# A hybrid decoder layer on one core: two weight tiles at the start, later scales, four products out, two weight tiles kept

## The chip, the cores and the metric

The kernel runs on one core of one Trainium2 chip. A core has five engines that each work through a queue of their own: TensorE (PE: matrix products; PEld is its loading of the stationary operand), VectorE (DVE), ScalarE (ACT), GpSimd (POOL) and SyncE (SP, which issues most transfers here). They wait for each other through semaphores, and 16 DMA engines carry the transfers. The metric is the time of one execution on the device in microseconds (us), smaller is better.

## The reference

One layer of a decoder, 1024 positions by 1024 channels, in float32:

```python
h = rms_norm(x, g_mix)
va, ga, xb, gb, sa, sb = split(h @ w_in + b_in)         # 1024, 1024, 1536, 1536, 1024, 1024 columns
u = silu(layer_norm(causal_conv31(va * sigmoid(ga)), ln_g, ln_b))
y_a = u @ w_a_out
v = rg_lru(causal_conv4(xb), ...)                       # gated linear recurrence along the positions
y_b = (v * gelu(gb)) @ w_b_out
x = x + (sigmoid(sa) * y_a + sigmoid(sb) * y_b) @ w_o
f = square(relu(rms_norm(x, g_mlp) @ w_1))              # 4096 columns
out = rms_norm(x + f @ w_2, g_final)
```

In rms_norm each row is divided by the root of its mean square and multiplied by a gain per channel. The decay of the recurrence needs softplus(-lam), a vector of 1536 values.

## The kernel before, in words

Activations lie with channels on the 128 partitions and positions along the free axis, so a product has a 128x128 weight block as its stationary operand and 512 positions moving. To keep float32 accuracy every operand is split into a high part (rounded to fp32r, suffix h) and a low part (the rest, suffix l), and each product is made three times: high by high ("hh"), low weight by high activation ("lh"), high weight by low activation ("hl").

The program has stages: the first three tiles of `w_in` (written out by hand, the code shown below), the rest of `w_in`, with a scheme of seven products in place of eight for some pairs of tiles (called z products from line 900 on), the output projections, the MLP's up projection (seven products again, numbered 1 to 7, in `up_step`), and its down projection. Inside a `manual_schedule` block the order on TensorE, VectorE and ScalarE is the order of the code; later stages keep clocks of their own (`at`, `later`, `fill`) by which VectorE's work is placed between the rest. Every engine works strictly in its order.

*The start.* SyncE loads a small vector of gains (`gmix`), the first weight tile `w0`, the first half of the positions of x transposed (four tiles `xc`, two blocks of 128 channels each), then `w1`, `w2`, and then x itself with positions on partitions (`x4` to `x7`, the first half of the positions; then the second half of `xc`, then `x0` to `x3`). TensorE runs idle passes (`idle_mm`, each float32 pass of 128x128 counting as two instructions in the trace). ScalarE makes `w0`'s high part and `xh`, VectorE the low parts, and TensorE multiplies as they come: all of tile z0 (24 products), then z1, then z2, always for the first half of the positions. These first products use x times the gain alone, without the root mean square, which is multiplied in later.

*The scales.* The root mean squares of the second half in time come from `x4` to `x7`: `x_square` squares a tile and sums along its row (on ScalarE, line 195), `x_root` turns the four sums into reciprocal roots on VectorE and ScalarE (v at line 202, diagonal matrices `rd` at 208 and 210), and `x_spread` spreads them over all partitions by four products with a matrix of ones (line 217, eight instructions in the trace). `x_scaled` then scales `xc` by that and ScalarE makes the next `xh` of it. In the same place `decay_on(n)` puts the next n steps of the softplus on VectorE, small operations of 12 columns on `sm` (lines 273 to 299).

*Guard products.* In the z products, banks b and e of a pair are first written by a ScalarE copy of another bank and then added to by products. For the first two pairs `z_bank` has a product write each of these banks ahead of the copy (line 918); nothing reads what it wrote.

*The up weights.* Tile i of the MLP's up projection uses two weight tiles of 512 KB, `w_{2i}` and `w_{2i+1}` (`raws[i, 0]`, `raws[i, 1]`). The stage ahead of it reads `raws[i, 0]` for i = 0 to 3, as the left operand of seven-product tiles named gu, gs ("u" in `g_lhs`). For i = 2 and 3 `g_lhs` forgets the tile afterwards, and the loop over the tiles loads whatever is missing:

```python
up_load(i, [m_ for m_ in (0, 1) if (i, m_) not in raws])
```

A split of an up weight is made by ScalarE and by an accumulating transfer that GpSimd issues (`split_dma`, line 66: `o<-s`).

Of the kernel before, what the change touches and what calls it, by code (L numbers as in the profile page):

```python
# [30 lines left out]
def trunk_kernel(ctx: ExitStack, tc: tile.TileContext, x, xt_in, xt_eo, vecs, w_in, w_a_out, w_b_pl, w_b_sq,  # L31
                 w_rg, w_o, w_1, w_2, g_final, out):

    nc = tc.nc
# [19 lines left out]
    HALVES = (slice(0, HS), slice(HS, S))  # L54


    def load_w(w, name):

        raw = wp.tile(list(w.shape), F32, tag="raw", name=name + "_raw")
        nc.sync.dma_start(raw, w)  # L60
        return raw
# [56 lines left out]
    wp = stage.enter_context(tc.tile_pool(name="weights", bufs=2))  # L118
# [8 lines left out]
    vec = cp.tile([P, 448], F32, name="vec")  # L127

    gmix = cp.tile([P, 16], F32, name="gmix")
    nc.sync.dma_start(gmix[:, 0:8], vecs[:, 0:8])  # L130
    nc.gpsimd.dma_start(vec, vecs)
    gmix_c = gmix[:, 0:8]
    bin_c = vec[:, 8:64]
# [11 lines left out]
    xt, xc, raw0 = [], [], []  # L145
# [6 lines left out]
    def load_xc(hf, c2):  # L152
        a = T(f"xc{hf}{c2}")
        nc.sync.dma_start(a, xt_in[hf, c2])
        xc.append(a)

    def load_w0(i):
        if i < 2:
            raw0.append(load_w(w_in[(16, 0, 8)[i]], f"w{i}"))
        else:  # L160
            raw0.append(T(f"w{i}_raw").rearrange("p (k c) -> p k c", c=P))
            nc.sync.dma_start(raw0[i], w_in[(16, 0, 8)[i]])

    load_w0(0)
    for c2 in range(4):
        load_xc(0, c2)
    load_w0(1)
    load_w0(2)
    for t in range(4, 8):
        load_x(t)  # L170
# [2 lines left out]
    for t in range(4):  # L173
# [3 lines left out]
    xh = [[(X1 if hf == 0 and c2 < 2 else T)(f"xh{hf}{c2}", F32R) for c2 in range(4)]  # L177
          for hf in range(2)]
    xl = [[T(f"xl{hf}{c2}", F32R) for c2 in range(4)] for hf in range(2)]

    def xpart(a, hf, c):
        return a[hf][c // 2][:, HALVES[c % 2]]

    rs_x = {}

    def x_square(t, eng):

        hf, i = divmod(t, 4)
        if hf not in rs_x:
            rs_x[hf] = cp.tile([P, 5, 4], F32, tag="st4", name=f"stx{hf}", bufs=2)  # L190
        a, ss = xt[(t + 4) % 8], rs_x[hf][:, 0, i:i + 1]
        if eng is nc.vector:
            nc.vector.scalar_tensor_tensor(a, a, 1.0, a, ALU.mult, ALU.mult, accum_out=ss)
        else:
            nc.scalar.activation(a, a, AF.Square, accum_out=ss)
# [16 lines left out]
    def x_spread(hf):  # L212

        rb[hf] = rb["tile"][:, HALVES[hf]]
        for i in range(4):
            d = slice(i * P, (i + 1) * P)
            nc.tensor.matmul(rb[hf][:, d], ones, rb["d"][:, d], start=True, stop=True)
# [6 lines left out]
    def x_plain(c):  # L224

        u = xc[c // 2][:, HALVES[c % 2]]
        nc.scalar.activation(xpart(xh, 0, c), u, AF.Copy, scale=gmix_c[:, c:c + 1])

    def x_plain_low(c):
        u, h = xc[c // 2][:, HALVES[c % 2]], xpart(xh, 0, c)  # L230
        nc.vector.scalar_tensor_tensor(xpart(xl, 0, c), u, gmix_c[:, c:c + 1], h.bitcast(F32),
                                       ALU.mult, ALU.subtract)
# [8 lines left out]
    w0 = []  # L241

    def first_w(i, part):
        if part == "h":
            if i < 2:
                wh = wp.tile([P, 8, P], F32R, tag="wh", name=f"w{i}_h")
                wl = wp.tile([P, 8, P], F32R, tag="wl", name=f"w{i}_l")
            else:
                wh, wl = (T(f"w{i}_{n}", F32R).rearrange("p (k c) -> p k c", c=P) for n in "hl")
            w0.append((wh, wl))  # L250
            z0.append(PS(f"z{16 + i}"))
            nc.scalar.activation(wh, raw0[i], AF.Copy)
        else:
            nc.vector.tensor_tensor(w0[i][1], raw0[i], w0[i][0].bitcast(F32), ALU.subtract)

    def first_z(i, hf, k, which):
        w, a = {"hh": (0, xh), "lh": (1, xh), "hl": (0, xl)}[which]
        nc.tensor.matmul(z0[i][:, HALVES[hf]], w0[i][w][:, k, :], xpart(a, hf, k),  # L258
                         start=k == 0 and which == "hh",
                         stop=k == 7 and which == ("hl" if i == 0 else "lh"))  # L260
# [69 lines left out]
    def decay_on(n=99):  # L330

        for _ in range(n):
            next(decaying, None)

    with tc.manual_schedule(engines={mybir.EngineType.Activation, mybir.EngineType.DVE,
                                     mybir.EngineType.PE}):
        warm = cp.tile([P, 10], F32, name="warm")
        nc.vector.memset(warm[:, 0:2], 1.0)
        nc.scalar.activation(warm[:, 0:1], warm[:, 1:2], AF.Sqrt)

        spare = PS("spare", "ps2")

        def idle_mm(n):
            for _ in range(n):
                nc.tensor.matmul(spare[:, 0:P], ones, ones, start=True, stop=True)

        idle_mm(13)
        rb["tile"] = PS("rb", "ps2")
        first_w(0, "h")
        first_w(0, "l")  # L350
        for c in range(8):
            x_plain(c)
            x_plain_low(c)
            if c == 7:
                first_w(1, "h")
                first_w(1, "l")
            for which in ("hh", "lh", "hl"):
                first_z(0, 0, c, which)
        for k in range(8):
            first_z(1, 0, k, "hh")  # L360
            first_z(1, 0, k, "hl")
        decay_on(6)
        first_w(2, "h")
        first_w(2, "l")
        decay_on(14)
        for t in range(4, 8):
            x_square(t, nc.scalar)
        for k in range(8):
            first_z(1, 0, k, "lh")
        x_root(1)  # L370
        decay_on(5)
        for k in range(8):
            first_z(2, 0, k, "hh")
            first_z(2, 0, k, "hl")
            if k == 4:
                x_spread(1)
        for k in range(8):
            first_z(2, 0, k, "lh")

        for c in range(9):  # L380
            if c < 8:
                x_scaled(1, c)
            else:
                x_root(0)
                x_spread(0)
            if 3 <= c < 7:
                x_square(c - 3, nc.scalar)
# [399 lines left out]
    for i in range(2, NZ):  # L787
        n = zseq.index((i, 1))
# [20 lines left out]
    with tc.manual_schedule(engines=ENGINES):  # L809
        for s in range(3, NC1):  # L810
# [30 lines left out]
            c = CH[s - 1]  # L841
# [27 lines left out]
            for d in range(5):  # L869
                if s - d in EXP:  # L870
# [6 lines left out]
                    t = 3 * g + d - (2 if g < 3 else 1)  # L877
# [21 lines left out]
    wp = stage.enter_context(tc.tile_pool(name="weights2", bufs=3, reuse_waits="tile"))  # L899
# [13 lines left out]
    hgd = dp.tile([12, P, S], F32, name="hgd")  # L913
    def z_bank(i, b):
        zb[i, b] = t = zp.tile([P, HS], F32, tag="z", name=f"z{i}{b}")
        if i < 2 and b in "be":

            nc.tensor.matmul(t, xh[0][0][:, 0:P], xh[0][0][:, 0:HS], start=True, stop=True)
        return t

    def z_mm(i, p):
# [101 lines left out]
    with tc.manual_schedule(engines=ENGINES):  # L1023
# [159 lines left out]
        for n in range(len(zseq) + 2):  # L1183
# [9 lines left out]
            if n + 3 < len(zseq):  # L1193
                i, p = zseq[n + 3]
# [15 lines left out]
    wp = early.enter_context(tc.tile_pool(name="weights3", bufs=7, reuse_waits="tile"))  # L1210
# [191 lines left out]
    def g_lhs(w, i, p):  # L1402
        if w == "u":
            src = raws[i, 0][:, 4 * (p - 1):4 * p, :]
            if p == 2 and i > 1:
                del raws[i, 0]
        elif p in (5, 6):
            src = gs[w, i][p - 5 and 1]
        else:
            src = graw[w, i, {1: 0, 2: 1, 3: 1, 7: 0, 4: 1}[p]][:, int(p == 4)]  # L1410
        go[w, i, p] = o = T(f"g{w}{i}_{p}", F32R).rearrange("p (x k c) -> p x k c", x=2, c=P)
        if w == "a" and p in (1, 2, 7):
            nc.scalar.activation(o[:, 0], src, AF.Copy)
# [242 lines left out]
    raws = {}  # L1656
# [300 lines left out]
    with tc.manual_schedule(engines={mybir.EngineType.Activation, mybir.EngineType.DVE,  # L1957
                                     mybir.EngineType.PE}):
        for n in range(len(useq)):
# [4 lines left out]
            while ready < min(len(useq), n + look + 1):  # L1964
                i, p = useq[ready]
# [167 lines left out]
    with tc.manual_schedule(engines={mybir.EngineType.Activation, mybir.EngineType.DVE,  # L2133
                                     mybir.EngineType.PE}):
        for n, (g, p, kk) in enumerate(dseq[:-2]):
# [41 lines left out]
            if (g, m - 4) in XADD:  # L2177
                k = XADD[g, m - 4]
# [103 lines left out]
```

## Time and profile before

| | us |
|---|---|
| median of three runs (lowest, highest) | 1531.57 (1530.81, 1531.60) |
| the profiled execution | 1531.15 |
| its span, first to last instruction | 1529.4 |
| TensorE busy | 1519.5, 99%, 6722 instructions |
| VectorE busy | 1200.0, 78%, 1636 instructions |
| ScalarE busy | 928.3, 61%, 1299 instructions |
| GpSimd busy | 192.3, 13%, 228 instructions |

The granted TensorE clock is 0.999 of full speed over the span. In a timeline a row gives the start, the duration, the engine, the line, the operation, out<-in, the shape, and in brackets how long the engine stood idle before it and what released it. Successive matmuls overlap, so the distance between their starts says more than their duration. A row of the DMA view names the queue's transfers, their number and size and the median time from issue to landing.

### The profile page before, as it was taken

To read this page: it belongs to the slowest core of one execution; us is meant where nothing else is said; L and a number is where in the kernel's file an instruction comes from. 1 tells how busy PE (TensorE), PEld (TensorE's weight loads), DVE (VectorE), ACT (ScalarE), POOL (GpSimd) and SP (SyncE) were. 2 spreads that over 40 slices of the span, in tenths; PEclk is the share of its full clock that TensorE was granted. 3 is DMA by queue.
4 is the path that set the end of the run, shared out by engine and by line. 5 is a ranking of instruction groups with operands and counts; after the bars stand their busy time and mean duration, and the time that the engine had idled before them with its cause. 6 is when DMAs were issued, how large, how long until landed. Compare 5 with 4: busy or idle time off the path is not lost.

```text
span 1529.4 us, 18963 instructions
## 1 busy us (share of the span) xinstructions
PE 1519.5 (99%) x6722; PEld 1251.2 (82%) x6722; DVE 1200.0 (78%) x1636; ACT 928.3 (61%) x1299; POOL 192.3 (13%) x228
## 2 busy tenths in 40 slices
PE   9999999999999999999999999999999999999998
PEld 7878887888888888888888887888888888888886
DVE  6899996998999997788869879755555387777777
ACT  6748688576566667645575777554444455545475
POOL 0111011022222222000022332000000000101010
PEclk9999999999999999999999999999999999999999
DMA  9766779797997889964879897333333974776465
GB/s 352 188 146 154 184 159 204 196 258 209 265 261 173 186 207 271 297 226 119 269 201 302 188 205 195 138 122 111 111 111 111 302 265 131 177 211 169 107 123 153
DMA packets 130799, 296.53 MB, mean 194 GB/s; under 512 B 12896, under 2 KB 34912, under 8 KB 130704
## 3 DMA queue, kind: packets, MB, share of 16 engines
q1 hardware_dynamic: 98960, 215.92, 42.0%
q0 software_dynamic: 31600, 79.15, 28.1%
q8 instruction: 52, 0.85, 0.2%
q14 instruction: 43, 0.35, 0.1%
q10 hardware_dynamic: 144, 0.26, 0.0%
HBM read 149.79 MB, written 60.82 MB: 138 GB/s over the span
## 4 chain that ended last, share of the span: by engine, by line
PE 96%; issue 2%; DVE 1%; POOL 1%; DMA 0%; ACT 0%; POOLq 0%; ACTq 0%
PE z L725 16%; PE z L258 2%; PE d1b L2002 2%; PE d2b L2002 2%; PE d0b L2002 2%; PE d3b L2002 2%; PE d0e L2002 1%; PE d3e L2002 1%; PE d3a L2002 1%; PE d2e L2002 1%; PE d2a L2002 1%; PE d1e L2002 1%; PE d1a L2002 1%; PE d0a L2002 1%; PE rg L532 1%
## 5 line engine op out<-in xcount | busy, mean ns | idle before, releaser
L725 PE MATMUL z<-xh,win_h 128*128 128x512 f32 x368 | 115.4, 391 | 0.0
L725 PE MATMUL z<-xl,win_h 128*128 128x512 f32 x368 | 114.9, 390 | 0.0
L637 DVE SCALAR_TENSOR_TENSOR y<-u,vec,y 128x511 f32<-128x511 f32 (+14 forms) x120 | 88.2, 735 | 0.0
L725 PE MATMUL z<-xh,win_l 128*128 128x512 f32 x368 | 87.4, 389 | 0.0
L637 DVE SCALAR_TENSOR_TENSOR yt<-u,vec,yt 128x511 f32<-128x511 f32 (+6 forms) x112 | 82.5, 736 | 0.0
L637 DVE SCALAR_TENSOR_TENSOR y<-yt,csum,y 128x511 f32<-128x511 f32 (+6 forms) x112 | 82.4, 736 | 0.0
L725 PEld LDWEIGHTS z<-xh,win_h 128*128 128x128 f32 x368 | 69.1, 188 | 16.0 <-ACT win_h L67 0.5
L725 PEld LDWEIGHTS z<-xl,win_h 128*128 128x128 f32 x368 | 69.1, 188 | 14.9
L725 PEld LDWEIGHTS z<-xh,win_l 128*128 128x128 f32 x368 | 69.1, 188 | 14.6
L542 ACT ACTIVATE g<-rg,vec 96x1024 f32<-96x1024 f32 x32 | 35.5, 1110 | 72.9 <-PE rg L534 72.8
L1697 ACT ACTIVATE o<-s 128x512 fp32r<-128x512 f32 x56 | 33.7, 623 | 45.7 <-DVE s L1681 26.4
L66 POOL DMA_DIRECT2D zo<-zw x45 | 39.2, 871 | 133.8 <-ACT zo L65 110.4
L483 DVE SCALAR_TENSOR_TENSOR v<-xb,vec,v 128x1023 f32<-128x1023 f32 (+2 forms) x36 | 46.2, 1282 | 6.3 <-ACT v L474 5.3
L66 POOL DMA_DIRECT2D db_10l<-br x4 | 3.5, 877 | 339.6 <-DMA br<-in_w_dram 254.4
L66 POOL DMA_DIRECT2D win_l<-win_raw x23 | 20.0, 868 | 194.0 <-ACT win_l L65 155.9
L65 ACT ACTIVATE zo<-zw 128x512 fp32r<-128x512 f32 x45 | 28.2, 626 | 24.3 <-PE z10f L929 2.1
L1219 DVE TENSOR_TENSOR o<-s,o 128x512 fp32r<-128x512 f32 x56 | 37.2, 683 | 1.3 <-ACT o L1697 1.3
L66 POOL DMA_DIRECT2D zo<-zs x30 | 26.4, 879 | 75.9 <-ACT zo L65 63.8
L67 ACT ACTIVATE zo<-zw 128x512 fp32r<-128x512 f32 x45 | 27.9, 621 | 0.0
L578 DVE TENSOR_TENSOR_SCAN g<-a,g 128x1024 f32<-128x1024 f32 x12 | 27.5, 2291 | 0.4
L66 POOL DMA_DIRECT2D ga<-gsa x8 | 7.0, 874 | 161.0 <-DMA m<-mbd 150.8
L1219 DVE TENSOR_TENSOR o<-w_raw,o 128x512 fp32r<-128x512 f32 x38 | 25.9, 683 | 0.0
(3182 smaller groups left out, 4912.0 us busy)
## 6 DMA issues: line engine op xcount, KB each, us to landing
w_raw<-in_w_dram SPq DMA_DIRECT2D x34, 512.0 KB, 5.7
br<-in_w_dram SPq DMA_DIRECT2D x32, 512.0 KB, 6.1
ar<-fd SPq DMA_DIRECT2D x32, 512.0 KB, 7.0
zw<-in_w_in_dram SPq DMA_DIRECT2D x28, 512.0 KB, 6.9
win_raw<-in_w_in_dram SPq DMA_DIRECT2D x23, 512.0 KB, 5.0
win_l<-win_raw POOLq DMA_DIRECT2D x23, 512.0 KB, 5.2
zo<-zw POOLq DMA_DIRECT2D x45, 256.0 KB, 5.7
gates<-zg SPq DMA_DIRECT2D x32, 256.0 KB, 4.1
```

Of the source, the lines that this page charges most:

```text
L65: nc.scalar.activation(l, src, AF.Copy, scale=-1.0)
L66: nc.gpsimd.dma_start(l, src, accum_op=ALU.add)
L67: nc.scalar.activation(h, src, AF.Copy)
L258: nc.tensor.matmul(z0[i][:, HALVES[hf]], w0[i][w][:, k, :], xpart(a, hf, k), start=k == 0 and which == "hh", stop=k == 7 and which == ("hl ...
L483: nc.vector.scalar_tensor_tensor(v[:, d:S], a[:, 0:S - d], cbw_c[:, w * 12 + t:w * 12 + t + 1], v[:, d:S], ALU.mult, ALU.add)
L542: nc.scalar.activation(a, gps.pop((n, gi))[:HD, :], AF.Sigmoid, bias=(ba_c, bx_c)[gi][:, n:n + 1])
L578: nc.vector.tensor_tensor_scan(i, a, i, 0.0, ALU.mult, ALU.add)
L637: nc.vector.scalar_tensor_tensor(o[:, k:], a[:, 0:HS - k], c, o[:, k:], ALU.mult, add)
L725: nc.tensor.matmul(zps[s][:, HALVES[hf]], w[:, k, :], xw[k][part][hf], start=n == 0, stop=n == 23)
L1219: tt(l, src, h.bitcast(F32), ALU.subtract)
L1697: nc.scalar.activation(o[:, 0], src, AF.Copy)
L2002: nc.tensor.matmul(o, a, b, start=start and n == 0, stop=stop and n == len(todo) - 1, skip_group_check=not start or not stop)
```

## The change

There are four groups of edits.

1. *Loads and first products.* `w0`, `w1` and the first `xc` tile are loaded in halves; `gmix` and the first half of `xc00` are issued by ScalarE. The idle passes go from 13 to 10 calls. Weights `w0` and `w1` are split by halves, and z0's and z1's products are interleaved, two blocks of channels at a time.
2. *Scales.* The square of `x6` is made by VectorE, the squares stand ahead of `decay_on(14)`, and the spread of the first scales stands after all 16 hh and hl products of z2 instead of after ten.
3. *Guard products.* The product in `z_bank` is gone.
4. *Up weights.* `g_lhs` keeps `raws[2, 0]` and `raws[3, 0]`, so tiles `w_4` and `w_6` aren't loaded a second time.

```diff
-    nc.sync.dma_start(gmix[:, 0:8], vecs[:, 0:8])
...
-    load_w0(0)
-    for c2 in range(4):
-        load_xc(0, c2)
-    load_w0(1)
+    def half_w0(i, n):
+        k = slice(4 * n, 4 * n + 4)
+        nc.sync.dma_start(raw0[i][:, k], w_in[(16, 0)[i], :, k])
+
+    half_w0(0, 0)
+    nc.scalar.dma_start(xc[0][:, HALVES[0]], xt_in[0, 0, :, HALVES[0]])
+    nc.scalar.dma_start(gmix[:, 0:8], vecs[:, 0:8])
+    nc.sync.dma_start(xc[0][:, HALVES[1]], xt_in[0, 0, :, HALVES[1]])
+    half_w0(1, 0)
+    load_xc(0, 1)
+    half_w0(0, 1)
+    half_w0(1, 1)
+    load_xc(0, 2)
+    load_xc(0, 3)
     load_w0(2)
     for t in range(4, 8):
         load_x(t)
...
-    def x_square(t, eng):
+    def x_square(t, dve=False):
...
-        if eng is nc.vector:
+        if dve:
             nc.vector.scalar_tensor_tensor(a, a, 1.0, a, ALU.mult, ALU.mult, accum_out=ss)
         else:
             nc.scalar.activation(a, a, AF.Square, accum_out=ss)
...
+    def first_half(i, n):
+        k = slice(4 * n, 4 * n + 4)
+        h, l = (a[:, k] for a in w0[i])
+        nc.scalar.activation(h, raw0[i][:, k], AF.Copy)
+        nc.vector.tensor_tensor(l, raw0[i][:, k], h.bitcast(F32), ALU.subtract)
...
-        idle_mm(13)
+        idle_mm(10)
         rb["tile"] = PS("rb", "ps2")
         first_w(0, "h")
-        first_w(0, "l")
+        first_w(1, "h")
+        first_half(0, 0)
         for c in range(8):
             x_plain(c)
             x_plain_low(c)
-            if c == 7:
-                first_w(1, "h")
-                first_w(1, "l")
+            if c == 1:
+                first_half(1, 0)
+            elif c == 3:
+                first_half(0, 1)
+                first_half(1, 1)
             for which in ("hh", "lh", "hl"):
                 first_z(0, 0, c, which)
-        for k in range(8):
-            first_z(1, 0, k, "hh")
-            first_z(1, 0, k, "hl")
+            if c % 2:
+                for k in (c - 1, c):
+                    first_z(1, 0, k, "hh")
+                    first_z(1, 0, k, "hl")
         decay_on(6)
         first_w(2, "h")
         first_w(2, "l")
+        for t in range(4, 8):
+            x_square(t, t == 6)
         decay_on(14)
-        for t in range(4, 8):
-            x_square(t, nc.scalar)
         for k in range(8):
             first_z(1, 0, k, "lh")
         x_root(1)
         decay_on(5)
         for k in range(8):
             first_z(2, 0, k, "hh")
             first_z(2, 0, k, "hl")
-            if k == 4:
+            if k == 7:
                 x_spread(1)
         for k in range(8):
             first_z(2, 0, k, "lh")
...
     def z_bank(i, b):
         zb[i, b] = t = zp.tile([P, HS], F32, tag="z", name=f"z{i}{b}")
-        if i < 2 and b in "be":
-
-            nc.tensor.matmul(t, xh[0][0][:, 0:P], xh[0][0][:, 0:HS], start=True, stop=True)
         return t
...
             src = raws[i, 0][:, 4 * (p - 1):4 * p, :]
-            if p == 2 and i > 1:
-                del raws[i, 0]
```

Lines of the kernel after are shifted by some 15 to 16 from before. On VectorE, where the scales are made (`sm` are the steps of the decay, `stx` the sums and roots), before:

```order
L254 TENSOR_TENSOR w_l<-w_raw,w_h 128x1024
L286 SCALAR_TENSOR_TENSOR sm<-sm 128x12
L288 SCALAR_TENSOR_TENSOR sm<-sm 128x12
L290 MEMSET sm 128x12
L293 TENSOR_TENSOR sm<-sm 128x12
...
L293 TENSOR_TENSOR sm<-sm 128x12
L202 TENSOR_SCALAR stx_261<-stx_261 128x4
```

and after:

```order
L264 TENSOR_TENSOR w_l<-w_raw,w_h 128x1024
L202 SCALAR_TENSOR_TENSOR x_112,stx_251<-x_112 128x1024
L302 SCALAR_TENSOR_TENSOR sm<-sm 128x12
L304 SCALAR_TENSOR_TENSOR sm<-sm 128x12
L306 MEMSET sm 128x12
L309 TENSOR_TENSOR sm<-sm 128x12
...
L309 TENSOR_TENSOR sm<-sm 128x12
L211 TENSOR_SCALAR stx_251<-stx_251 128x4
```

The square of x6 (`x_112`) has come in ahead of the 14 decay steps, of which the first four and the last are shown; the first step of the roots (v, line 202 before, 211 after) stands behind them as it did.

On TensorE, at the end of z2's first half (`z_244` before, `z_248` after), before:

```order
L258 MATMUL z_244<-xh_131,w_h 128x512
L258 MATMUL z_244<-xl_139,w_h 128x512
L217 MATMUL rb<-rd_281,ones 128x128 x4
L258 MATMUL z_244<-xh_131,w_h 128x512
L258 MATMUL z_244<-xl_139,w_h 128x512
...
L258 MATMUL z_244<-xh_132,w_h 128x512
L258 MATMUL z_244<-xl_140,w_h 128x512
L258 MATMUL z_244<-xh_129,w_l 128x512 x2
```

and after:

```order
L274 MATMUL z_248<-xh_135,w_h 128x512
L274 MATMUL z_248<-xl_143,w_h 128x512
L226 MATMUL rb<-rd_285,ones 128x128 x4
L274 MATMUL z_248<-xh_132,w_l 128x512 x2
L274 MATMUL z_248<-xh_133,w_l 128x512 x2
L274 MATMUL z_248<-xh_134,w_l 128x512 x2
L274 MATMUL z_248<-xh_135,w_l 128x512 x2
L274 MATMUL z_171<-xh_136,w_h 128x512
```

The last row of after (`z_171`) is the first product of the second half of the positions. The spread (`rb<-rd`) has moved behind six more products; 8 products are left between it and the second half where there were 14.

On SyncE, at the beginning of the up projection (`fd` are its results, written out), before:

```order
L1486 DMA fd<-f_3_8066 128x512
L1664 DMA w_4_raw<-in_w_dram 128x1024
L1664 DMA w_5_raw<-in_w_dram 128x1024
L1664 DMA w_6_raw<-in_w_dram 128x1024
L1766 DMA fd<-fa_8152 128x512
L1664 DMA w_7_raw<-in_w_dram 128x1024
```

and after:

```order
L1501 DMA fd<-f_3_8066 128x512
L1679 DMA w_5_raw<-in_w_dram 128x1024
L1679 DMA w_7_raw<-in_w_dram 128x1024
L1781 DMA fd<-fa_8152 128x512
L1679 DMA w_8_raw<-in_w_dram 128x1024
```

The loads of w_4 and w_6 are gone, and w_5, w_7 and w_8 have moved up against the results.

More of the change, by code (lines that the diff above doesn't have):

```diff
@@ L157, in load_w0 @@
     def load_w0(i):
[L158 to L162, printed above, removed]
-    load_w0(0)
-    for c2 in range(4):
-        load_xc(0, c2)
-    load_w0(1)
+        raw0.append(T(f"w{i}_raw").rearrange("p (k c) -> p k c", c=P))
+        nc.sync.dma_start(raw0[i], w_in[(16, 0, 8)[i]])
+    raw0 += [wp.tile([P, 8, P], F32, tag="raw", name=f"w{i}_raw") for i in range(2)]
+    xc.append(T("xc00"))
+    def half_w0(i, n):
[11 more added lines that the diff above has]
+    load_xc(0, 3)
     load_w0(2)
@@ L251, in first_w @@
             z0.append(PS(f"z{16 + i}"))
-            nc.scalar.activation(wh, raw0[i], AF.Copy)
+            if i == 2:
+                nc.scalar.activation(wh, raw0[i], AF.Copy)
         else:
             nc.vector.tensor_tensor(w0[i][1], raw0[i], w0[i][0].bitcast(F32), ALU.subtract)
+    def first_half(i, n):
[3 more added lines that the diff above has]
+        nc.vector.tensor_tensor(l, raw0[i][:, k], h.bitcast(F32), ALU.subtract)
     def first_z(i, hf, k, which):
@@ L386, in trunk_kernel @@
             if 3 <= c < 7:
-                x_square(c - 3, nc.scalar)
+                x_square(c - 3)
             if c:
```

## The prediction

> **What bounds the kernel now.** I read the page first (span, busy shares, the chain that ended last), then TensorE's timeline at the three places that the change touches, then ScalarE, VectorE and the DMA queues there.
>
> ```profile
> span 1529.4 us, 18963 instructions
> ...
> PE 1519.5 (99%) x6722; PEld 1251.2 (82%) x6722; DVE 1200.0 (78%) x1636; ACT 928.3 (61%) x1299; POOL 192.3 (13%) x228
> ...
> PE 96%; issue 2%; DVE 1%; POOL 1%; DMA 0%; ACT 0%; POOLq 0%; ACTq 0%
> ```
>
> TensorE is busy for 99% of the span and carries 96% of the chain. So an edit counts in two ways only: it takes matmuls off TensorE, or it shortens one of its few waits. The first such place is the start:
>
> ```profile
> 1.60 5.92 PE L345 MATMUL spare<-ones 128*128 128x128 f32 x26 [1.60 <-POOL ones L113]
> 7.17 0.70 PE L258 MATMUL z<-xh,w_h 128*128 128x512 f32 x1
> ...
> 17.12 1.98 PE L258 MATMUL z<-xh,w_l 128*128 128x512 f32 x8
> 18.94 0.39 PE L258 MATMUL z<-xh,w_h 128*128 128x512 f32 x1
> ...
> 20.98 0.39 PE L258 MATMUL z<-xl,w_h 128*128 128x512 f32 x1
> 21.50 1.13 PE L217 MATMUL rb<-rd,ones 128*128 128x128 f32 x8
> 22.38 0.47 PE L258 MATMUL z<-xh,w_h 128*128 128x512 f32 x1
> 22.70 0.39 PE L258 MATMUL z<-xl,w_h 128*128 128x512 f32 x1
> ...
> 25.66 0.39 PE L258 MATMUL z<-xh,w_h 128*128 128x512 f32 x1
> ...
> 36.77 1.05 PE L217 MATMUL rb<-rd,ones 128*128 128x128 f32 x8
> 37.58 0.48 PE L258 MATMUL z<-xh,w_h 128*128 128x512 f32 x1
> ```
>
> Eight products from 17.12 to 18.94 give the undisturbed step, 1.82 / 8 = 0.2275 us. From the first product (7.17) to the first of the third tile (18.94) stand 48 products, 10.92 us at that step, in 11.77: 0.85 us is lost there. The first spread takes 22.38 - 20.98 - 0.23 = 1.17 us, the second, which waits for nothing, 37.58 - 36.77 = 0.81. The second half of the positions begins at 25.66; all that the start gains must be seen there.
>
> **The start.** The idle passes fall from 26 to 20. One takes 5.92 / 26 = 0.228, so TensorE is free 6 x 0.228 = 1.37 us earlier, near 5.8. The data must be there too:
>
> ```profile
> 0.74 0.39 SPq L130 DMA_DIRECT2D gmix<-in_vecs_dram  x1
> 1.18 0.42 SPq L60 DMA_DIRECT2D w_raw<-in_w_in_dram  x1
> ...
> 4.95 1.06 ACT L252 ACTIVATE w_h<-w_raw 128x1024 fp32r<-128x1024 f32 x1 [2.72 <-DMA w_raw<-in_w_in_dram]
> 6.34 1.33 ACT L227 ACTIVATE xh<-xc,gmix 128x512 fp32r<-128x512 f32 x2 [0.34 <-DMA xc<-in_xt_dram]
> ```
>
> The first weight tile is issued in gmix's place, 1.18 - 0.74 = 0.44 earlier, and its half is half the copy (0.53 for 1.06); before, its bytes had landed by 4.95. An estimate of 5.9 for the first product follows, 1.27 earlier. Two tiles side by side give TensorE ten products per pair of halves of xc (2.28 us) where one tile gave six (1.37) against ScalarE's 1.33, so much of the 0.85 should go as well. TensorE then comes to the moved spread after 64 products, at 5.9 + 14.56 = 20.5, or 21.1 with 0.6 lost. By itself that is 1.3 to 2.1 us gained. It counts only if the scales are there.
>
> **The scales.** Their chain before:
>
> ```profile
> 17.09 1.06 ACT L195 ACTIVATE x<-x 128x1024 f32<-128x1024 f32 x1 [0.15 <-DMA x<-in_x_dram]
> ...
> 18.36 1.06 ACT L195 ACTIVATE x<-x 128x1024 f32<-128x1024 f32 x1
> 19.33 0.18 ACT L195 ACTIVATION_READ_ACCUMULATOR x<-x 128x1 f32 x1
> ...
> 23.45 0.63 ACT L222 ACTIVATE xh<-xc 128x512 fp32r<-128x512 f32 x1 [1.70 <-DVE xc L221]
> ```
>
> ```profile
> 16.31 0.17 DVE L286 SCALAR_TENSOR_TENSOR sm<-sm 128x12 f32<-128x12 f32 x1
> ...
> 18.80 0.17 DVE L293 TENSOR_TENSOR sm<-sm 128x12 f32<-128x12 f32 x1
> 19.54 0.17 DVE L202 TENSOR_SCALAR stx<-stx 128x4 f32<-128x4 f32 x1 [0.58 <-ACT x L195]
> ...
> 24.11 0.69 DVE L236 TENSOR_TENSOR xl<-xc,xh 128x512 fp32r<-128x512 f32 x1
> ```
>
> The squares on ScalarE start as x6 and x7 land (17.09, 18.36); the 14 decay steps on VectorE lie in their shadow, and v (19.54) waits 0.58 for the last square. The change turns this round: on VectorE the square of x6 stands ahead of the 14 steps, and v behind them. VectorE works in order, so it sits until x6 is there, and the steps, v, the roots and the diagonals queue behind. The steps take 18.80 - 16.31 + 0.20 = 2.69 us. The square on VectorE has no row; the nearest forms are
>
> ```profile
> L483 DVE SCALAR_TENSOR_TENSOR v<-xb,vec,v 128x1023 f32<-128x1023 f32 (+2 forms) x36 | 46.2, 1282 | 6.3 <-ACT v L474 5.3
> ...
> q1 hardware_dynamic: 98960, 215.92, 42.0%
> ...
> q1 hardware_dynamic: 1739, 6.34, 98.8%
> ```
>
> so 1.28 us for the same operation and width, the lower end; the upper is 1.46, with 0.18 for reading the sum as ScalarE's row does. I take 1.28, the row of its own engine. The other two rows bound the landing of x6 (queue, packets, MB, share of 16 engines). The first is the whole span, 0.42 x 1529.4 x 16 / 98960 = 104 ns for a packet of 2.18 KB, 48 ns per KB; the second the stretch 4 to 20, 0.988 x 16 x 16 / 1739 = 145 ns for 3.65 KB, 40 per KB. That queue is full, so x6 lands when the bytes ahead of it have passed. They stay the same, and the stream starts up to 0.44 earlier; but 768 rows of 2 KB replace 384 of 4 KB, which costs between nothing (same price per byte) and 384 x 4.1 KB x 8 ns / 16 engines = 0.8 us. I take 0.3, nearer to the lower end, since the mean over the span holds many small packets. x6 is then ready at 17.09 - 0.44 + 0.3 = 16.95, between 16.65 and 17.45, and v at 16.95 + 1.28 + 2.69 = 20.92, 1.38 later than before.
>
> Behind v nothing changes: 22.38 - 19.54 = 2.84 to the next product. After the moved spread only 8 products are left before the second half, where there were 14: 0.32 + 7 x 0.2275 = 1.91. The second half begins at v + 4.75 = 25.67, against 25.66. The first xh of that half is ready at 24.08 - 19.54 = 4.54 behind v, its low part at 24.80 - 19.54 = 5.26, needed 4.75 + 0.46 = 5.21 behind it: 0.05 of wait, within what I can tell. So TensorE arrives early and waits some 1.8 us at the spread: **the start is worth 0**, from +0.3 (x6 at 16.65) to -0.7 (17.45, and the square 1.46). The two other edits here (earlier first products, the later place of the spread) have their whole gain taken by this wait.
>
> A place for the Trainium skill: VectorE: DVE Perf Modes, section "Two Vector instructions with no wait between them", says that an operation which also writes out its accumulator is two instructions, the main one and an accumulator read. No VectorE row here shows it; by it and ScalarE's 0.18 the start would come to -0.2 and the sum to 1529.8 in place of 1529.6.
>
> **The guard products.** They are whole-width products that write to a bank nobody reads:
>
> ```profile
> 340.00:366.00 26.00, 26.00 (x116) 21.53 (x115) 24.24 (x35) 17.29 (x28) 4.38 (x5) 1.00 0.81 204
> ...
> L918 PE MATMUL z1e<-xh x1: 389/389/389, 364.3 to 364.3; 128*128 128x512 f32 x1
> ```
>
> From 340 to 366, where all four stand (this is the last), TensorE is busy for 26.00 us of 26.00: it waits for nothing there, and each guard takes a step. Four of them: 4 x 0.2275 = **0.91 us**. The copies of ScalarE that waited for a guard now wait for the product ahead of it, one step sooner. What could eat it is a buffer or a load that comes at a fixed time; I bound it by 0.7 and 0.91 and take 0.91.
>
> **The up weights.** Two loads of 512 KB fall away, w_4 and w_6; before, w_4, w_5 and w_6 were issued from 938.81 on:
>
> ```profile
> 937.92 0.87 POOL L66 DMA_DIRECT2D o<-s  x1 [0.65 <-ACT o L65]
> ...
> 938.81 6.63 SPq L1664 DMA_DIRECT2D w_raw<-in_w_dram  x3
> ...
> 940.95 1.22 DVE L1219 TENSOR_TENSOR gu7l<-x,gu7h 128x1024 fp32r<-128x1024 f32 x1 [1.03 <-ACT gu7h L1369]
> ...
> 944.28 0.39 PE L1709 MATMUL f0d<-gu7l,o 128*128 128x512 f32 x1
> 945.45 0.73 PE L1709 MATMUL f0d<-gu7h,o 128*128 128x512 f32 x2 [0.77 <-DMA o<-s]
> 946.02 0.39 PE L1709 MATMUL f0d<-gu7l,o 128*128 128x512 f32 x1
> ...
> o<-s POOLq DMA_DIRECT2D x2, 256.0 KB, 3.7
> ...
> o<-s POOLq DMA_DIRECT2D x1, 256.0 KB, 7.5
> ```
>
> TensorE stands between 944.28 and 945.45, 0.94 more than a step, and the next two products take 0.57 for 0.455, 0.11 more: 1.05 us, for an accumulating transfer that POOL issued at 937.92. Two such transfers issued before the loads landed in 3.7 us, this one in 7.5. Now w_4 is in place and w_5 is the first load. It takes the buffer that VectorE's low part of gu7 frees, which ends at 940.95 + 1.22 = 942.17. By then 937.92 + 3.7 = 941.6 has passed, and TensorE wants the data at 944.51. So the stall goes: **1.05 us**, at least 0.9 if the restart keeps its 0.11. Late next would be w_5: issued at 942.2, it is there at 949.7 with the 7.5 above; VectorE's sums for the next tile must not want it sooner, or the stall moves there.
>
> **Sum.** 0 + 0.91 + 1.05 = 1.96 us off the profiled execution, 1531.15 (span 1529.4 and 1.7 around it): 1529.2. It lies 0.42 below the median of the runs, 1531.57, so on the median 1529.6; by its bounds (+0.3 to -0.7; 0.91 to 0.7; 1.05 to 0.9) 1529.3 to 1530.7.
>
> **Rivals.**
> *The scales are not late.* If x6 lands by 15.4, the decay steps are over before x7's square, which ends v's wait at 18.36 - 0.14 + 0.97 + 0.18 = 19.4; the second half begins at 24.15, 1.5 earlier, and the time is 1531.57 - 3.46 = 1528.1. For it speaks TensorE's early arrival; against it the full queue, which cannot bring x6 1.7 us forward by a start 0.44 earlier.
> *The up stall stays.* If the transfer is slow because others of its kind follow it, not because of the loads, or if w_5 is issued sooner than I think, 1.05 is not gained: 1530.7. For it: no row says what holds the transfer up. Against it: 3.7 beside 7.5.
> *Slower: half rows at the price of whole ones.* Then 384 more packets of 4.1 KB x 40 = 163 ns each, over 16 engines, put x6 off by 3.9 us, to 20.55; v is at 24.5, and the start loses 3.6, together 1531.57 + 3.6 - 1.96 = 1533.2. From a landing at 18.9 on the loss outweighs the rest. Against it: the span's mean packet, 104 ns for 2.18 KB.
> *The clock drops in the wait.* At half clock for one window of 3.4 us TensorE loses 1.7: 1531.3. The row of before shows no drop with a gap of 1.17:
>
> ```profile
> 18.90:25.60 6.70, 6.57 (x33) 5.29 (x33) 5.12 (x19) 2.88 (x8) 0.00 (x0) 1.00 1.03 408
> ```
>
> (the clock is the 1.00 ahead of the last two numbers). The Trainium skill, TensorE: Matmul & The Clock Gate, section "Part 1: The HAM clock gate", says that an idle window of about 3.4 us halves the clock; by that rule a wait of 1.8 us stays below it, and the trace agrees as far as its 1.17 goes.
>
> **Chances.** The forecast 0.68; scales in time 0.13; up stall stays 0.12; dear half rows 0.04; clock 0.03. Run to run the kernel before varied by 0.8 us, so I give the forecast's own range as 1528.9 to 1530.9; with the two likelier rivals the range is 1528.0 to 1531.3. 0.2% is 3.06 us, about what separates two times of this kernel: faster means below 1528.5 (0.10 of the first rival, 0.03 of the forecast's edge), slower above 1534.6 (0.02, the third rival made worse), the rest 0.85 lies between.
>
> **What would show it.** Right: a wait of TensorE of 1.5 to 2 us just ahead of the first spread, with v behind the decay steps near 20.9; the second half at 25.4 to 26.4; no guard rows; no gap at f0d, its transfer landed in under 5 us. Wrong: the spread reached without a wait, x6 ready outside 16.6 to 17.5, an f0d stall of more than 0.3, or a new gap of TensorE elsewhere.

## The result and the profile after

The changed kernel takes 1529.23 us (median of 21 runs, 1528.77 to 1530.64), the kernel before, run beside it, 1531.34 (21 runs, 1530.44 to 1532.3). The ratio is 0.9986, with a 95% interval of 0.998 to 0.9993: 2.1 us faster, between 1.1 and 3.1. The forecast was 1.96 us less, 1529.6.

The page of the kernel after: span, busy times, and the chain that ended last.

```profile
span 1527.2 us, 18954 instructions
...
PE 1517.7 (99%) x6712; PEld 1249.8 (82%) x6712; DVE 1200.8 (79%) x1640; ACT 927.0 (61%) x1299; POOL 192.3 (13%) x228
...
PE 98%; DMA 1%; DVE 0%; issue 0%; SPq 0%; ACT 0%; DVEq 0%
```

TensorE is the bound as before; its busy time fell by 1.8, its instructions by 10 (4 guards, 6 idle passes). At the start its timeline reads:

```profile
6.14 0.79 PE L274 MATMUL z<-xh,w_h 128*128 128x512 f32 x1
...
21.66 0.39 PE L274 MATMUL z<-xl,w_h 128*128 128x512 f32 x1
22.71 1.13 PE L226 MATMUL rb<-rd,ones 128*128 128x128 f32 x8 [0.67 <-DVE rd L217]
23.60 2.09 PE L274 MATMUL z<-xh,w_l 128*128 128x512 f32 x8
25.53 0.39 PE L274 MATMUL z<-xh,w_h 128*128 128x512 f32 x1
25.76 0.40 PE L274 MATMUL z<-xh,w_l 128*128 128x512 f32 x1
26.08 0.50 PE L274 MATMUL z<-xl,w_h 128*128 128x512 f32 x1
```

The first product is 1.03 earlier than before (7.17), but the second half begins at 25.53 against 25.66: 0.13 is left. The rest went at 22.71, where TensorE waits for the scales (22.71 - 21.66 - 0.23 = 0.82). And even the 0.13 is given back: the first product with a low part comes 0.09 late at 26.08, the next steps are longer, and from there to the end of the first stage this profile runs 0.14 behind that of before (the product that starts at 53.96 there starts at 54.10 here). VectorE shows why the scales are late:

```profile
17.05 1.22 DVE L202 SCALAR_TENSOR_TENSOR x<-x 128x1024 f32<-128x1024 f32 x1 [0.78 <-DMA x<-in_x_dram]
18.20 0.08 DVE L202 DVE_READ_ACCUMULATOR x<-x 128x1 f32 x1
18.20 0.16 DVE L302 SCALAR_TENSOR_TENSOR sm<-sm 128x12 f32<-128x12 f32 x1
...
20.68 0.17 DVE L309 TENSOR_TENSOR sm<-sm 128x12 f32<-128x12 f32 x1
20.77 0.16 DVE L211 TENSOR_SCALAR stx<-stx 128x4 f32<-128x4 f32 x1
```

It waits 0.78 for x6, squares it, runs the 14 decay steps, and only then takes v, at 20.77 (19.54 before). (The tiles x4 to x7 hold the second half of the positions, the half whose scales are made here.) At the up projection the transfer that f0d waits for, the products behind it, and that transfer's group among the issues of its moment (median time to landing at the end):

```profile
937.13 0.87 POOL L66 DMA_DIRECT2D o<-s  x1 [0.65 <-ACT o L65]
```

```profile
943.30 0.39 PE L1724 MATMUL f0d<-gu7l,o 128*128 128x512 f32 x1
943.52 0.62 PE L1724 MATMUL f0d<-gu7h,o 128*128 128x512 f32 x2
```

```profile
o<-s POOLq DMA_DIRECT2D x1, 256.0 KB, 4.0
```

It lands after 4.0 us, not 7.5, and the gap is gone (943.52 - 943.30 is one step). Between the two profiles the last product starts 2.09 earlier: 0.91 of the guards, 1.05 at f0d, 0.18 at two small gaps near 925 that the second profile lacks, less the 0.14 of the start, which makes 2.00.

### The profile page after: what moved, and what is told of

It is laid out like the page before. It is cut to its first block, busy times and chain, and to the rows that moved or that the text cites. A ratio compares the mean times of both kernels' runs of the same rounds, so it can differ in the third digit from the quotient of the medians.

```text
span 1527.2 us, 18954 instructions
## 1 busy us (share of the span) xinstructions
PE 1517.7 (99%) x6712; PEld 1249.8 (82%) x6712; DVE 1200.8 (79%) x1640; ACT 927.0 (61%) x1299; POOL 192.3 (13%) x228
## 4 chain that ended last, share of the span: by engine, by line
PE 98%; DMA 1%; DVE 0%; issue 0%; SPq 0%; ACT 0%; DVEq 0%
PE z L745 16%; PE d1b L2017 2%; PE d2b L2017 2%; PE d0b L2017 2%; PE d3b L2017 2%; PE d0e L2017 1%; PE d0a L2017 1%; PE d3e L2017 1%; PE d3a L2017 1%; PE d1e L2017 1%; PE d1a L2017 1%; PE d2e L2017 1%; PE d2a L2017 1%; PE z L274 1%; PE rg L552 1%; PE rg L554 1%
```

## The experiments

Theory: the start is worth nothing, because the square of x6 and the decay steps hold up the scales; guards and up weights carry the gain with 0.91 and 1.05. Against it: that the start gains and the others give something back, that TensorE's own start or the landing of the tiles sets the second half, and that the stall at f0d is not the loads' doing.

**One part at a time.** The guards alone:

```diff
--- before
-        if i < 2 and b in "be":
-            nc.tensor.matmul(t, xh[0][0][:, 0:P], xh[0][0][:, 0:HS], start=True, stop=True)
```

> The kernel before without the four guard products, nothing else changed. Theory (each is one step of TensorE and nothing waits for it in any other way): TensorE has 8 instructions fewer in the trace or 4 products fewer, everything behind 365 us lies 0.91 us earlier, the span is 0.9 shorter, the time 0.9 less (0.9994 of before). Rival (a buffer or a load at a fixed time takes the gain back): a new gap of TensorE of 0.2 us or more behind 342, and a span less than 0.5 shorter.

Measured: 1530.84 against 1531.50, ratio 0.9997 (0.9988 to 1.0006), 0.66 less where 0.91 was expected; the interval includes no change, so the times alone show nothing here. TensorE has 4 instructions fewer. Its busy time falls by 1.0, but that is no measure of the guards: three profiles of the kernel before have 1519.5, 1519.0 and 1518.5. A better one is the distance from a product ahead of the first guard to one behind the last, in the kernel before and in the kernel after:

```profile
339.12 0.39 PE L929 MATMUL z0a<-xh,zo 128*128 128x512 f32 x1
372.67 0.39 PE L929 MATMUL z2a<-xh,zo 128*128 128x512 f32 x1
```

```profile
339.26 0.39 PE L946 MATMUL z0a<-xh,zo 128*128 128x512 f32 x1
371.90 0.39 PE L946 MATMUL z2a<-xh,zo 128*128 128x512 f32 x1
```

It is 33.55 in all five profiles with the guards and 32.64 in all nine without, this one among them: 0.91, four steps. The span of the guards alone, though, is 0.6 longer than that of the kernel before in its first profile, by three gaps, where that profile had none at z10f and f1d and 0.18 at gu1a:

```profile
549.97 0.72 PE L926 MATMUL z10f<-xs4h,zo 128*128 128x512 f32 x2 [0.84 <-DMA zo<-zw]
...
926.60 0.73 PE L1424 MATMUL gu1a<-gu2h,gu 128*128 128x512 f32 x2 [1.03 <-DMA gu<-w_raw]
...
948.88 0.72 PE L1706 MATMUL f1d<-gu7h,o 128*128 128x512 f32 x2 [0.22 <-DMA o<-s]
```

All three are waits for accumulating transfers. That looks like the rival, a gain taken back; but at f0d, where the kernel before stood for 1.05, this one has no gap, with the same loads beside it. One profile of each was not enough to say which gaps belong to which kernel; the repeats of before, below, settle that. The up weights alone:

```diff
--- before
-            if p == 2 and i > 1:
-                del raws[i, 0]
```

> The kernel before with w_4 and w_6 kept, nothing else changed. Theory (the loads of w_4 and w_5 hold up the accumulating transfer that TensorE waits for): the transfer issued at 937.9 lands in under 5 us, TensorE's gap of 0.93 at 944.3 and the 0.11 behind it are gone, the time is 1.05 less (0.9993 of before). Rival (the accumulating transfers hold each other up): they are issued at the same distances as before, so the gap stays, and so does the time.

Measured: 1530.24 against 1531.50, ratio 0.9992 (0.9983 to 1.0001), 1.26 less, with an interval that just includes no change. No gap at f0d or f1d, though the accumulating transfers are issued at the same distances as before; the one for f0d lands after 5.4 us, a little over the 5 I gave it, and early enough. A gap of 0.52 stands at 400, where before had none. The start alone:

```diff
--- after
+        if i < 2 and b in "be":
+            nc.tensor.matmul(t, xh[0][0][:, 0:P], xh[0][0][:, 0:HS], start=True, stop=True)
...
+            if p == 2 and i > 1:
+                del raws[i, 0]
```

> The changed kernel with the guard products and the second loads of w_4 and w_6 put back: the edits of the start alone, against the kernel before. Theory (the square of x6 and the 14 decay steps hold the scales, and TensorE waits at the spread): the second half of the positions begins at 25.5 as against 25.66, and the time is 0.1 less, not to be told from before. Rival (the start carries a gain and the other parts give less than their count): 0.5 to 1.5 less.

Measured: 1531.99 against 1531.50, ratio 1.0003 (0.9994 to 1.0012): no gain, rather a loss. The rival falls. On VectorE and TensorE:

```profile
17.46 1.23 DVE L202 SCALAR_TENSOR_TENSOR x<-x 128x1024 f32<-128x1024 f32 x1 [0.79 <-DMA x<-in_x_dram]
```

```profile
25.94 0.39 PE L274 MATMUL z<-xh,w_h 128*128 128x512 f32 x1
```

x6 came 0.41 later than in the kernel after, with the same loads, and the second half 0.41 later.

**What holds the scales.** The square of x6 back on ScalarE, all else as changed:

```diff
--- after
-            x_square(t, t == 6)
+            x_square(t)
```

> The changed kernel with the square of x6 back on ScalarE, all else as changed. Theory (VectorE waits for x6 and the decay steps queue behind it): the decay steps run from 16.3 to 19.0 in the time in which x6 and x7 are awaited, v follows the square of x7 at 19.5 instead of 20.8, TensorE reaches the spread at 21.9 and waits less than 0.2 there, the second half begins at 24.6 instead of 25.53, and the time is 0.9 less than the changed kernel's (about 1528.3, 0.998 of before). Rival (the landing of the tiles or TensorE's own start sets the second half): it stays at 25.5 within 0.2, and so does the time.

Measured: 1528.19 against 1531.50, ratio 0.9979 (0.997 to 0.9988). The decay steps run while the tiles are awaited, and v follows the last square:

```profile
19.62 0.17 DVE L211 TENSOR_SCALAR stx<-stx 128x4 f32<-128x4 f32 x1 [0.67 <-ACT x L204]
```

```profile
21.74 0.39 PE L274 MATMUL z<-xl,w_h 128*128 128x512 f32 x1
21.97 1.05 PE L226 MATMUL rb<-rd,ones 128*128 128x128 f32 x8
22.77 2.08 PE L274 MATMUL z<-xh,w_l 128*128 128x512 f32 x8
24.69 0.39 PE L274 MATMUL z<-xh,w_h 128*128 128x512 f32 x1
```

TensorE takes the spread one step after its last product, without a wait, and the second half begins at 24.69, 0.84 before the kernel after. This is the theory's number, and the lowest median of the study. A second time, beside the last experiment below:

> The changed kernel with the square of x6 on ScalarE a second time, to be compared with the next kernel on the same chip, and for the start's landing times: x6 lands anywhere from 17.0 to 18.3 (seven profiles of starts by halves so far), TensorE never waits more than 0.2 at the spread, the second half begins 7.6 behind that landing (24.69 - 17.1). Time 0.9975 to 0.9985 of before.

Measured: 1528.56 against 1531.27, ratio 0.9981 (0.9972 to 0.999), second half at 24.89, again no wait. x6 landed at 17.33, so 7.6 ahead of it, as expected. That distance is not set by the scales, since TensorE doesn't wait for them here: it reaches the spread 0.20 later than in the first profile (22.17 against 21.97), as x6 lands 0.20 later. It wasn't run on one chip with the kernel after; each was set against before, and the two intervals overlap with that of 0.9986. That it is faster by 0.8 rests on the place in the trace, twice, more than on the clock.

The order on VectorE alone, with the square left there:

```diff
--- after
+        decay_on(14)
         for t in range(4, 8):
             x_square(t, t == 6)
-        decay_on(14)
```

> The changed kernel with the 14 decay steps ahead of the squares; the square of x6 stays on VectorE, behind them. Theory (the order on VectorE sets v): the steps run from 16.2 to 18.9, the square from there to 20.1, v starts near 20.1 to 20.3 (20.77 in the changed kernel, 19.6 with the square on ScalarE), the second half begins at 24.8 to 25.0, between the 25.53 and the 24.69 of those two. Rival (only the engine that squares x6 matters, since x6 lands late there): v at 20.8 and the second half at 25.5 again.

```profile
20.65 0.17 DVE L211 TENSOR_SCALAR stx<-stx 128x4 f32<-128x4 f32 x1
```

```profile
22.20 0.39 PE L274 MATMUL z<-xl,w_h 128*128 128x512 f32 x1
22.61 1.13 PE L226 MATMUL rb<-rd,ones 128*128 128x128 f32 x8
...
25.42 0.40 PE L274 MATMUL z<-xh,w_h 128*128 128x512 f32 x1
```

Taken as they stand, v at 20.65 and the second half at 25.42 lie nearer to the rival's numbers (20.8 and 25.5) than to the theory's. But in this execution x6 landed at 17.59, 0.57 later than in the kernel after, and w2 0.55 later, so the steps ended later as well. TensorE comes to the spread at 22.43 and waits 0.18 there, where the kernel after waits 0.82. Counted from the landing of x6, the second half begins 7.83 behind it, against 8.50 in the kernel after (25.53 less a landing at 17.02): 0.67 for the order on VectorE. That is an estimate, which takes the whole stream of loads to be late by the same amount; x6 itself had been there for 1.7 us when it was squared, at 19.32. One profile only, which agrees with the theory by this count and does not show it by itself.

**The place of the spread, and the idle passes.**

```diff
--- after (two kernels, one line each)
-            if k == 7:
+            if k == 4:
                 x_spread(1)
...
-        idle_mm(10)
+        idle_mm(13)
```

> The changed kernel with the spread of the scales after ten products of z2 again. Theory (TensorE waits for the scales wherever the spread stands): the spread begins at 22.7 as in the changed kernel, TensorE stands before it for 2.2 us instead of 0.8, 14 products follow in place of 8, and the second half begins 6 x 0.2275 = 1.37 later, at 26.9. Rival (the wait at the spread is short of what it costs, the place is without effect): 25.5 to 25.8.

```profile
20.28 0.39 PE L274 MATMUL z<-xl,w_h 128*128 128x512 f32 x1
22.71 1.13 PE L226 MATMUL rb<-rd,ones 128*128 128x128 f32 x8 [2.04 <-DVE rd L217]
...
26.89 0.39 PE L274 MATMUL z<-xh,w_h 128*128 128x512 f32 x1
```

As expected: the spread at 22.71 whatever stands ahead of it, a wait of 2.2 in place of 0.8, and the second half at 26.89. With the square of x6 where the change puts it, the later place of the spread saves 1.36; it repairs what the square costs.

> The changed kernel with 26 idle passes again. Theory (what TensorE gains at the start is lost at the spread): the first product starts at 7.1 to 7.2 instead of 6.14, TensorE reaches the spread near 22.7 and does not wait, the second half begins at 25.5 to 25.8, at most 0.3 later than in the changed kernel, while the first product is 1.0 later. Rival (earlier products count in full): 26.5.

```profile
6.87 0.47 PE L274 MATMUL z<-xh,w_h 128*128 128x512 f32 x1
...
23.78 1.13 PE L226 MATMUL rb<-rd,ones 128*128 128x128 f32 x8 [0.66 <-DVE rd L217]
24.67 2.08 PE L274 MATMUL z<-xh,w_l 128*128 128x512 f32 x8
26.58 0.39 PE L274 MATMUL z<-xh,w_h 128*128 128x512 f32 x1
```

```profile
18.11 1.23 DVE L202 SCALAR_TENSOR_TENSOR x<-x 128x1024 f32<-128x1024 f32 x1 [0.78 <-DMA x<-in_x_dram]
```

The second half at 26.58 is the rival's number, and TensorE waits at the spread where I expected no wait. But the idle passes did not do it: the first product is 0.73 later, the second half 1.05, and TensorE stands waiting in between. In this execution x6 was squared from 18.11 on, 1.06 later than in the kernel after, for reasons of the loads. In four kernels with the order of the kernel after, the second half begins at a fixed distance behind the square's start, whenever the first product was:

| | first product | square of x6 | second half | distance |
|---|---|---|---|---|
| after | 6.14 | 17.05 | 25.53 | 8.48 |
| the start alone | 6.35 | 17.46 | 25.94 | 8.48 |
| 26 idle passes | 6.87 | 18.11 | 26.58 | 8.47 |
| spread after ten products | 6.42 | 17.03 | 26.89 | 9.86 = 8.48 + 1.38 |

That shows the theory more sharply than the times do. How much of the landing at 18.1 is chance and how much the passes, one profile can't say; of the eight other starts by halves seven landed x6 earlier and one later.

**Is the stall at f0d a constant?** The kernel before, profiled twice more:

> The kernel before, unchanged, profiled a second time. Theory (the accumulating transfers land at times that differ by a microsecond or two between executions, and at f0d the time left is short when the loads run beside them): the transfer for f0d lands 6.4 to 7.5 us after its issue, TensorE's gap there is anything from 0 to 1.1, and gaps of the same kind stand or are missing at z10f near 549, at gu1a near 925 and at f1d near 948. Rival (the stall of 0.94 at f0d belongs to the program): it is there again within 0.2, and the other places have none.

> The kernel before, unchanged, profiled a third time; as for the second: a gap at f0d between 0 and 1.1 and others that come and go by the theory, the same 0.94 there and none elsewhere by the rival.

The two profiles, one row each:

```profile
948.10 0.74 PE L1709 MATMUL f1d<-gu7h,o 128*128 128x512 f32 x2 [0.47 <-DMA o<-s]
```

```profile
945.13 0.72 PE L1709 MATMUL f0d<-gu7h,o 128*128 128x512 f32 x2 [0.50 <-DMA o<-s]
```

The first has 0.26 at f0d and 0.74 at f1d, the second 0.77 at f0d and nothing behind it; the rival falls. All the profiles with the second loads, set beside those without (gaps with the long step behind each):

| | transfer for f0d, us to landing | gap at f0d | gap at f1d |
|---|---|---|---|
| before | 7.5 | 1.05 | 0 |
| before again, first | 6.5 | 0.26 | 0.74 |
| before again, second | 7.1 | 0.77 | 0 |
| guards alone | 6.4 | 0 | 0.49 |
| start alone | 6.7 | 0 | 0.42 |
| up weights alone | 5.4 | 0 | 0 |
| after | 4.0 | 0 | 0 |
| seven others with the weights kept | 3.9 to 4.3 | 0 | 0 |

With the loads the transfer takes 6.4 to 7.5 us and the two places cost 0.75 on average, between 0.42 and 1.05; without them it takes 3.9 to 5.4, and they cost nothing, in nine profiles of nine. So the loads are the cause, and 1.05 was the highest of five values. The two without a gap at f0d, guards alone and start alone, had stood 1.30 and 0.90 at gu1a just before, so TensorE came to f0d 7.2 and 6.8 us behind the transfer's issue, and in the kernel before 6.1. The gaps at z10f, gu1a and z3b come and go: in guards alone 1.11 and 1.30, in the start alone 0.81 and 0.90, with the weights kept between 0 and 1.0 in sum, in the kernel before 0.18, 0 and 0.11, in the kernel after 0. They stand in kernels with the guards and in kernels without. At z10f the traces say more: the transfer that it waits for is issued 9.2 us ahead of it in all fourteen profiles, with the guards or without, and a gap stands in the six in which that transfer took 9.59 or more to land, in none of the eight in which it took 9.40 or less. So that gap is not the price of taking the guards out.

**Two tries at a better start.** The gains ahead of xc on ScalarE's queue, and, in the second, the 224 KB vector loaded by SyncE between w2 and x4:

```diff
--- the kernel with x6 on ScalarE (two kernels)
+    nc.scalar.dma_start(gmix[:, 0:8], vecs[:, 0:8])
     nc.scalar.dma_start(xc[0][:, HALVES[0]], xt_in[0, 0, :, HALVES[0]])
-    nc.scalar.dma_start(gmix[:, 0:8], vecs[:, 0:8])
...
-    nc.gpsimd.dma_start(vec, vecs)
...
     load_w0(2)
+    nc.sync.dma_start(vec, vecs)
```

> The changed kernel with the square of x6 on ScalarE and with the gains issued ahead of the first half of xc on ScalarE's queue. Theory: the first xh no longer waits for the gains (they landed at 5.28, behind 2 KB rows) but for xc, which comes 0.2 to 0.4 sooner than that; the first product starts at 5.8 to 6.0, the second half begins at 24.3 to 24.6 (24.69 with the square alone), and the time is about 1528.0, 0.998 of before. Rival (xc lands as late as the gains did): no difference from the kernel with the square alone.

Measured: 1529.05 against 1531.21, ratio 0.9985 (0.9976 to 0.9994), not better. The first product does start at 5.89, but then TensorE stands for 1.23 behind the product of 7.25: w1's first half landed at 8.01, where it landed between 5.77 and 7.24 in the eight other starts by halves, and x6 at 18.31. Whether the order of the two transfers did that or chance, one profile doesn't show. What all queues carried from 4 to 8 us, in the kernel after and here:

```profile
DMA packets 799, 1.58 MB, mean 395 GB/s; under 512 B 222, under 2 KB 222, under 8 KB 799
```

```profile
DMA packets 458, 1.16 MB, mean 289 GB/s; under 512 B 69, under 2 KB 69, under 8 KB 458
```

> As the one before, and the vector of 224 KB that POOL loads at 1.5 us is loaded by SyncE between w2 and x4. Theory (the rows of this transfer, 1.8 KB from another queue, run among the first halves and take their engines' time): the first halves land 0.3 to 0.6 sooner, x6 at 16.9 to 17.1 without the spread to 18, the second half begins at 24.3 to 24.7, and the time is 0 to 0.5 below the kernel's beside it. Rival (the halves themselves make the stream uneven): x6 again between 17.0 and 18.3, and the same time.

Measured: 1528.38 against 1531.27, ratio 0.9981 (0.9972 to 0.999), the same as the kernel beside it. The first halves landed no sooner: w1's at 5.77 as in the kernel after, the second xc tile at 8.42 against 8.03. x6 landed at 18.01, but 0.59 of that is the vector itself, which now stands ahead of x4 in SyncE's queue (w2 landed at 13.58, the vector at 14.17). The second half began at 25.27. From 4 to 8 all queues carried 331 GB/s, which is less because the vector is missing from it: SyncE's queue carried 1.32 MB there, and 1.35 in the kernel after. So this profile gives no support to the theory that the vector's rows are to blame; it is one profile, set against landings that differ by up to 1 us between executions.

## Why the prediction was right, and where it was not

- **The bound** held: what counts is TensorE's work and its waits.
- **The start worth 0**: right within its range. One profile gives a loss of 0.14, the start alone a time between 0.9 less and 1.8 more. Further on, the first product of z0a starts between 339.07 and 339.28 in the five profiles of whole tiles, and at 339.26 and 339.65 in the two kernels with all edits of the start: 0.1 to 0.5 lost. The mechanism was the one named, by its rows: v at 20.77 (20.92 forecast), second half at 25.53 (25.67), and the kernel with x6 on ScalarE takes it away.
- **TensorE's arrival** at the spread was wrong in size: 21.89, not 20.5 to 21.1, since the first product came at 6.14 (5.9) and the products after it lost 1.2 us to data that was not there, not 0.6 at most. So the wait was 0.8 and not 1.8. The result does not notice, since the scales set the end. The price of an idle pass was one execution's value, too: the 26 took 5.92 in the profile that the prediction used, but 5.07 and 4.75 in its repeats, where TensorE then stood 0.63 and 0.79 for the first xh and the first product began at 7.30 and 7.14 all the same. There the data, not the passes, set the first product.
- **The low part of xh**: 0.05 of wait forecast; with its long steps it took 0.27 (from 0.13 ahead to 0.14 behind).
- **The square of x6 and the steps**: 1.28 taken for the square, 1.15 from its start to the next; 2.69 taken for the steps, 2.57 measured (18.20 to 20.77). The square started at 17.05, 0.10 later than forecast, so v came out close in part because errors cancelled. The reading of the sum stands as an instruction of its own, as the Trainium skill has it (VectorE: DVE Perf Modes, "Two Vector instructions with no wait between them"), but of 0.08, and the next step starts at the same 18.20: the 0.18 that I weighed for it was not there.
- **The landing of x6**: 16.95 forecast, 17.02 in the kernel after; the bounds 16.65 to 17.45 were too narrow. In the nine profiles of starts by halves it lies between 17.0 and 18.3; in the five of whole tiles between 17.0 and 17.2.
- **The guards**: 0.91 by the distance between products, in every profile; the times gave 0.66 with an interval that holds both.
- **The up weights**: the mechanism was right: VectorE's low part of gu7 ended at 941.39, w_5 was issued at 941.42, behind the transfer's landing (941.14), and f0d and f1d have no gap. The size was that of one execution, which lost 1.05; the mean of five is 0.75. This step took a measured stall for a constant.
- **Rivals.** The scales were late, as the forecast has it; an early v (19.62, where the first rival had 19.4) came about only when the square was moved back. The stall at f0d went. Half rows cost more than I took for them in some executions, but not what whole ones do. The clock stayed: the granted clock is 0.998 in the profile of the kernel after, with a wait of 0.8, and 0.999 in the one with the spread after ten products, with a wait of 2.2.

The sum of the parts as they are on average, 0.91 + 0.75 and a start of 0.1 to 0.5 lost, is 1.2 to 1.6; the time says 2.1, between 1.1 and 3.1. That the forecast of 1.96 lies so near is partly luck: it used the highest of five stalls, and the gaps elsewhere, which came to anything from 0 to 2.4 in one execution, were 0 in the kernel after.

## What to carry to other kernels

When an operation that must wait is put on an engine that works in order, look at what stands behind it: here a square that saved nothing by being moved took 14 small steps out of a time in which they were free, and swallowed the microsecond by which the first product had come earlier. Where an earlier start does not show, measure the end of the stage from the event that releases it, not from the clock: the distances of 8.48 told in four profiles what the times could not. And before a stall in one profile is booked as a gain, profile the same kernel again.

## What was not expected of the hardware

- *Loads by halves did not bring the stream forward, and made it uneven.* w0 is issued 0.44 earlier and its first half lands at 4.30 instead of the whole at 4.93, but x5 and x6 land when they did before (15.75 and 17.02 against 15.76 and 17.07), and in other executions of the same loads up to 1.1 later. The loss falls between 4 and 8 us: 328 to 400 GB/s there in seven profiles of the same loads, the lowest in the one with the latest x6, against 404 to 415 with whole tiles. Its cause is open; moving the vector's transfer out of the way did not help in one profile.
- *Accumulating transfers of 256 KB take between 3.3 and 11.2 us* from issue to landing (in the fourteen profiles), and the same transfer of the same program differs by about 1 us between executions: 6.5, 7.1 and 7.5 at f0d in the kernel before. TensorE's gaps in the long middle of the program, 0 to 2.9 us in all, are waits for such transfers; at f0d and z10f the traces show that they follow the time to landing.
